# Gate and up products of an adaLN block with retention, block attention and a convolved feed-forward: one 512-column product for high and low tokens, and exits spread over steps

## The chip, the cores and the metric

The kernel runs on one core of one Trainium2 chip, in one launch. The metric is device time in microseconds for one execution, read from the chip, as the median of several runs. All tensors are float32 at the borders. The chip's engines appear under these names: PE (TensorE, products), PEld (its weight loads), DVE (VectorE), ACT (ScalarE), POOL (GpSimd), SP (SyncE, which issues most DMA transfers).

## The reference

One block over 256 tokens of width 1024: a modulation computed from `c`, a token mixer (attention and retention, gated and projected), a layer norm, a feed-forward of width 2816 with a causal filter of three taps over the tokens, and a second layer norm. The change lies in the feed-forward:

```python
def conv_ffn(h, w_ff_gate, w_ff_up, ff_conv_w, ff_conv_b, w_ff_down):
    s = h.shape[1]
    g = h @ w_ff_gate
    u = h @ w_ff_up
    gp = jnp.pad(g, ((0, 0), (CONV_WIDTH - 1, 0), (0, 0)))
    g_conv = sum(gp[:, j:j + s, :] * ff_conv_w[j] for j in range(CONV_WIDTH)) + ff_conv_b
    a = jax.nn.gelu(g_conv, approximate=False) * u
    return a @ w_ff_down

def reference(...):
        ...
        x = layer_norm(DEEPNORM_ALPHA * x + g1 * y, ln1_g[l], ln1_b[l])
        h = x * (1.0 + sc2) + sh2
        y = conv_ffn(h, w_ff_gate[l], w_ff_up[l], ff_conv_w[l], ff_conv_b[l], w_ff_down[l])
        x = layer_norm(DEEPNORM_ALPHA * x + g2 * y, ln2_g[l], ln2_b[l])
```

## The kernel before

**Three products for one.** The products run in a rounded 32-bit type (`float32r`). To keep precision, each operand is split into a high part (rounded) and a low part (what the rounding lost), and `mm3` (L80) sums three products in one PSUM bank: high by high (L81), then the two mixed ones (L82, L83). The product of the two low parts is left out.

**Weights.** A list `main` holds the big weights in units of 128 x 2048 in the order of use. SP loads a unit into one of four `raw` buffers (`load_raw`, L70, issue on L74). Each unit has two halves of 128 x 1024. `prep_halves` splits a half: ACT writes `whi` (L1028), DVE writes `wlo` as raw minus `whi` (L1042); there are eight pairs of these (`HL_BUFS`). Once both halves of a raw buffer are split, the next load into it is issued.

**Steps.** `steps` is a list in which every step uses one half, or a few of them. The main loop at the end (from the line `for s, (need, rel, fn) in enumerate(steps)`) writes out the order of instructions by hand: for each step it advances side work, prepares halves as long as pairs are free (up to eight ahead), and then calls the step's function, which issues the products and, behind them, what takes the result out of the bank. Each engine works through its own queue in this order. In the feed-forward the side work is the scaling of the first norm's output for the second residual (L985), and the products of the last part of the modulation on DVE (`ada`, L154).

**Rounds.** The 2816 features of the feed-forward are 11 rounds of 256. In a round the gate weights and the up weights are stationary: a half has eight blocks of 128 x 128, index k over the 1024 inputs, and the tokens, 256 columns, stream through. `wstat8` (L306) puts the two halves of a unit in the two halves of one of four banks (P0 to P3, taken in turn by `one_bank`). For rounds 0 and 1 the up products run the other way round, with tokens stationary, before the rounds begin. The order of the units is: gate 0, gate 1, then gate r and up r, from round 2 on followed by the down unit of the round before (r = 2: down 0 and down 1) until round 7; rounds 8 to 10 have gate and up alone. The last four down units (rounds 7 to 10) follow as a tail: four steps for the first 128 tokens, one for each round, then three steps for the other 128. The down products have the features stationary and stream 512 columns of weights into banks P4 to P7.

**Exits.** After a gate unit, `gate_done` (L605) lets ACT compute tap 2 and the bias from the bank (L612, once for each half of 128 features), DVE add taps 1 and 0 (L615, four instructions), and ACT take Gelu (L617). After an up unit, `act_in` (L623) multiplies the bank by the gate's result on DVE (L625), and splits the product into `ah` (ACT, L66) and `al` (DVE, L67), the stationary operands of the down unit. All of these are issued at once behind the unit's last product.

**Tokens.** The high and low tokens of the feed-forward lie in four buffers A3a, A3b (high, k 0 to 3 and 4 to 7) and A6a, A6b (low). Earlier stages use the same buffers for other things: input columns, rotated queries and keys, `rv`, the mixer's output; the tail uses A6a and A6b as scratch.

Of the kernel before, what the change touches and what calls it, by code (L numbers as in the profile page):

```python
# [7 lines left out]
F32 = mybir.dt.float32  # L8
F32R = mybir.dt.float32r
AF = mybir.ActivationFunctionType  # L10
OP = mybir.AluOpType
# [17 lines left out]
T0_AT, XN, PRIME = 4, 256, 3  # L29
W0, W1, W2 = (4, 5), (6,), (7,)  # L30
PIECES = dict(ada1=[(0, 512, 1024, 2048)] + [2] * 3 + [1] * 4, winA=[4] * 2 + [2] * 2 + [1] * 4, winX=[1] * 2)
CHUNK = 2
BUSY = 3
SEQ = [(s[0], int(s[1])) for s in
# [17 lines left out]
def _body(nc, a, out, pe, act, dve, sp, cst, wts, big, tmp, ps, dram):  # L52
    f = lambda ap: ap.bitcast(F32)

    def bank(i):
        return ps.tile([128, 512], F32, tag=f"P{i}", name=f"P{i}")

    def slot(n, shape, dt=F32):
        return big.tile(shape, dt, tag=f"A{n}", name=f"A{n}")

    def halves(n):

        return [slot(n + e, [128, 4, 256], F32R) for e in "ab"]
# [16 lines left out]
    def mm3(o, lh, ll, rh, rl, start, stop):  # L80
        pe.matmul(o, lh, rh, start=start, stop=False)  # L81
        pe.matmul(o, lh, rl, start=False, stop=False)  # L82
        pe.matmul(o, ll, rh, start=False, stop=stop)  # L83

    def table(func):

        d_ = tmp.tile([128, 1], F32, name="dummy", bufs=1)
        act.activation(d_, epst, func)
# [7 lines left out]
    consts = {}  # L96
# [5 lines left out]
    bcol = first[:, 136:].rearrange("p (s j) -> p s j", s=6)  # L102
    mod = cst.tile([128, 6, 8], F32, name="mod")

    raws = {}
    loads_A = [(dict(a="ada1", W="winA", X="winX")[n], j) for n, j in SEQ if n in "aWX"]

# [141 lines left out]
    main = []  # L249
# [41 lines left out]
    def one_bank():  # L291
        i = bank_i[0]
        bank_i[0] = (i + 1) % 4
        return bank(i)
# [11 lines left out]
    def wstat8(name, u, xh, xl, done, mid=None):  # L306
        get = lazy(one_bank)

        def mk(half):
            def mm(hi, lo):  # L310
                if half and mid:
                    mid()
                p = get()
                for k in range(8):
                    mm3(p[:, half * 256:half * 256 + 256], hi[:, k * 128:(k + 1) * 128],
                        lo[:, k * 128:(k + 1) * 128], xh(k), xl(k), k == 0, k == 7)
                if half:
                    done(p)
            return mm
        weights(a[name][u], mk(0), mk(1))  # L320

    def wstat4(name, u, xh, xl, done):
# [9 lines left out]
            return mm  # L332
        weights(a[name][u], mk(0), mk(1))

    S = {}
    ghh, ghl = (lambda k: hh[:, k]), (lambda k: hl[:, k])

# [200 lines left out]
        weights4(src, [mk(0, 0), mk(0, 1), mk(1, 0), mk(1, 1)], [range(4)] * 4)  # L538

    def out_start():  # L540
        S["h2h"], S["h2l"] = halves("3"), halves("6")
        GB = S["GB"] = tmp.tile([128, 2, 8], F32, name="GB", bufs=1)
        m = mod[:, 2:4]
        lncol = consts["lncol"]
        dve.tensor_tensor(GB[:, 0], lncol[:, 0], m[:, 0], OP.mult)
        dve.tensor_tensor(GB[:, 1], lncol[:, 1], m[:, 0], OP.mult)
        dve.tensor_tensor(GB[:, 1], GB[:, 1], m[:, 1], OP.add)
        table(AF.Sqrt)
# [56 lines left out]
    def gate_done(r):  # L605
        def fn(p):
            g = slot(("5", "15")[r % 2], [128, 2, 256])
            pv = p.rearrange("p (i t) -> p i t", i=2)
            convw = consts["convw"]
            w = lambda n, i: convw[:, n, 2 * r + i:2 * r + i + 1]  # L610
            for i in range(2):
                act.activation(g[:, i], pv[:, i], AF.Identity, scale=w(2, i), bias=w(3, i))  # L612
# [8 lines left out]
        return fn  # L621

    def act_in(r, u):  # L623
        g = S.pop(("gelu", r)).rearrange("p a b -> p (a b)")
        dve.tensor_tensor(g, u, g, OP.mult)  # L625
        ah = slot(("9a", "9b", "10a", "8a")[r % 4], [128, 2, 256], F32R)
        al = slot(("2a", "2b", "4", 0)[r % 4], [128, 2, 256], F32R)
# [42 lines left out]
    def tok0(i):  # L670
        def fn(ts):
            if i == 0:
                table(AF.Sqrt)
            for hf in range(2):
                down(NR - NG + i, 0, hf, ts[hf], BOTH, False, i == NG - 1 and hf == 1)
            if i == NG - 1:
                n = Norm(S["x1"][:, 0], S["g", 1], S["z2"][0], ("6a", "6b"))
                for c, w in BOTH:
                    n.piece(c, w, S["yf"][c // 512])
                S["rows"] = out_rows(n, 0, BOTH)  # L680
                next(S["rows"])
        return fn

    def tok1(c, w):
# [21 lines left out]
                    pass  # L706
        return fn

    def ffn_gate(r):
        wstat8("wgate", r, gh2, gl2, gate_done(r))  # L710

    def ffn_up(r):
        wstat8("wup", r - 2, gh2, gl2, up_done(r))

    def first():
        bank_i[0] = 0
# [175 lines left out]
    def retention():  # L892
# [50 lines left out]
        for g in range(HR + 1):  # L943
            yield
            if g:
                for t in range(2):
                    act.activation(yr[t][:, c], yr[t][:, c], AF.Copy, scale=sd[:, 2 * g + t - 2:2 * g + t - 1])
            if g < HR:
                c = slice(g * 256, (g + 1) * 256)
                for t in range(2):  # L950
                    dve.scalar_tensor_tensor(yr[t][:, c], yr[t][:, c], mv[:, 2 * g + t, 0:1], srg[t][:, c],
                                             op0=OP.subtract, op1=OP.mult)
            yield
            yield
        yrh, yrl = halves("3"), halves("6")
        S["yrh"], S["yrl"] = yrh, yrl
        for _ in range(3):
# [111 lines left out]
    def run_sides():  # L1069
        for g in list(sides):  # L1070
            if next(g, StopIteration) is StopIteration:
                sides.remove(g)

    for s, (need, rel, fn) in enumerate(steps):
        S["main"] = s
        if s == LN1_AT + 8:
            sides.append(residual())
        run_sides()
        prep_to(max(need) + 1, True)
        late = LN1_AT < s < LN1_AT + 8  # L1080
        if not late:
            prep_to(max(need) + 1 + (LOOKAHEAD if s < LN1_AT - 1 else HL_BUFS))
        run_sides()
        fn([tiles[h] for h in need])
        for h in rel:
            tiles.pop(h)
            live[0] -= 1
        while s % 2 and later and later[0][0] <= s:
            later.pop(0)[1]()
        run_sides()  # L1090
        if late and s >= LN1_AT + PRIME:
            if s == LN1_AT + PRIME:
                next(pg)
            elif s > LN1_AT + 4:
                prep_to(max(need) + 1 + HL_BUFS)
# [90 lines left out]
```

## Time and profile before

| | |
|---|---|
| median of 3 runs | 437.45 us (437.12 to 437.57) |
| the profiled execution's own time | 437.32 us |
| span of the profiled execution, first to last instruction | 435.5 us |
| mean granted TensorE clock | 0.997 |
| DMA | 105.72 MB, mean 243 GB/s |

The span is what the profiler's timeline covers; the profiled execution's own time is 1.8 us longer than its span. In a row of a view that groups instructions stand the line of the kernel, the engine, the operation, output<-inputs with their shapes, the count, the busy time and mean duration of one, and the idle time of the engine just before such instructions with what ended it. In a view of waits stand who waited for whom, the total, how often, and the longest. Products on PE overlap, so the mean duration of one is longer than the distance between two starts.

### The profile page before, as it was taken

To read this page: it belongs to the slowest core of one execution; us is meant where nothing else is said; L and a number is where in the kernel's file an instruction comes from. 1 tells how busy PE (TensorE), PEld (TensorE's weight loads), DVE (VectorE), ACT (ScalarE), POOL (GpSimd) and SP (SyncE) were. 2 spreads that over 40 slices of the span, in tenths; PEclk is the share of its full clock that TensorE was granted. 3 is DMA by queue.
4 is the path that set the end of the run, shared out by engine and by line. 5 is a ranking of instruction groups with operands and counts; after the bars stand their busy time and mean duration, and the time that the engine had idled before them with its cause. 6 is when DMAs were issued, how large, how long until landed. Compare 5 with 4: busy or idle time off the path is not lost.

```text
span 435.5 us, 6921 instructions
## 1 busy us (share of the span) xinstructions
PE 422.5 (97%) x2738; PEld 379.0 (87%) x2738; DVE 346.1 (79%) x550; ACT 241.7 (55%) x369; POOL 6.7 (2%) x16
## 2 busy tenths in 40 slices
PE   5999999999999999999999999999999999999993
PEld 2768888877788999999989899899999999999882
DVE  4979689979997999697779887798886665577476
ACT  4466578579774477543453995655445545355500
POOL 0000000100000000000000010000000000000000
PEclk9999999999999999999999999999999999999998
DMA  8999887787468778779672079577766784550001
GB/s 263 412 423 355 319 322 292 304 339 250 147 275 299 289 288 298 279 286 316 236 267 108 0 255 401 186 267 257 278 238 251 288 274 160 195 193 2 2 24 72
DMA packets 19696, 105.72 MB, mean 243 GB/s; under 512 B 2512, under 2 KB 4560, under 8 KB 8784
## 3 DMA queue, kind: packets, MB, share of 16 engines
q1 hardware_dynamic: 18288, 100.29, 62.1%
q0 software_dynamic: 1376, 4.99, 3.4%
q8 instruction: 21, 0.34, 0.3%
q14 instruction: 11, 0.09, 0.1%
HBM read 104.22 MB, written 1.06 MB: 242 GB/s over the span
## 4 chain that ended last, share of the span: by engine, by line
PE 92%; DMA 4%; DVE 2%; issue 1%; ACT 0%; SPq 0%; DVEq 0%
PE P L81 28%; PE P L82 28%; PE P L83 28%; DMA raw<-in_strm 3%; DMA A3b<-in_strm 1%; PE P L532 1%; PE P L534 1%; PE P L535 1%; PE P L776 1%; PE P L828 1%; PE P L847 1%; PE P L871 1%; DVE junk L154 1%; DVE wlo L67 0%; PE P L917 0%
## 5 line engine op out<-in xcount | busy, mean ns | idle before, releaser
L1042 DVE TENSOR_TENSOR wlo<-raw,whi 128x1024 fp32r<-128x1024 f32 x118 | 140.4, 1219 | 24.7 <-ACT whi L1028 24.7
L1028 ACT ACTIVATE whi<-raw 128x1024 fp32r<-128x1024 f32 x118 | 120.2, 1051 | 41.3 <-PE P L83 12.4
L83 PE MATMUL P<-whi,A 128*128 128x512 f32 (+1 forms) x212 | 80.3, 379 | 0.0
L81 PE MATMUL P<-whi,A 128*128 128x512 f32 (+1 forms) x168 | 65.4, 389 | 0.1
L82 PE MATMUL P<-wlo,A 128*128 128x512 f32 (+1 forms) x168 | 64.0, 381 | 0.5 <-DVE wlo L67 0.5
L154 DVE CUSTOM_DVE_ANT_0 junk<-raw,srow 128x1024 bf16<-128x1024 f32 (+1 forms) x49 | 58.7, 1197 | 3.5 <-ACT srow L141 1.8
L81 PE MATMUL P<-A3a,whi 128*128 128x256 f32 x192 | 54.4, 283 | 0.0
L81 PE MATMUL P<-A3b,whi 128*128 128x256 f32 x192 | 54.3, 283 | 0.0
L82 PE MATMUL P<-A6b,whi 128*128 128x256 f32 x192 | 54.3, 283 | 0.0
L83 PE MATMUL P<-A3b,wlo 128*128 128x256 f32 x192 | 54.3, 283 | 0.0
L83 PE MATMUL P<-A3a,wlo 128*128 128x256 f32 x192 | 54.3, 283 | 0.0
L82 PE MATMUL P<-A6a,whi 128*128 128x256 f32 x192 | 54.3, 283 | 0.0
L83 PEld LDWEIGHTS P<-whi,A 128*128 128x128 f32 x212 | 39.9, 188 | 7.9
L81 PE MATMUL P<-A,whi 128*128 128x256 f32 x160 | 45.9, 287 | 0.0
L83 PE MATMUL P<-A,wlo 128*128 128x256 f32 x160 | 45.2, 283 | 0.0
L82 PE MATMUL P<-A,whi 128*128 128x256 f32 x160 | 45.2, 283 | 0.0
L81 PEld LDWEIGHTS P<-whi,A 128*128 128x128 f32 x168 | 31.6, 188 | 7.1 <-issue 1.3
L82 PEld LDWEIGHTS P<-wlo,A 128*128 128x128 f32 x168 | 31.7, 188 | 6.7 <-DVE wlo L67 1.2
L82 PEld LDWEIGHTS P<-A6a,whi 128*128 128x128 f32 x192 | 36.8, 192 | 0.3
L81 PEld LDWEIGHTS P<-A3a,whi 128*128 128x128 f32 x192 | 36.8, 192 | 0.3
L81 PEld LDWEIGHTS P<-A3b,whi 128*128 128x128 f32 x192 | 36.9, 192 | 0.0
L82 PEld LDWEIGHTS P<-A6b,whi 128*128 128x128 f32 x192 | 36.9, 192 | 0.0
(235 smaller groups left out, 734.0 us busy)
## 6 DMA issues: line engine op xcount, KB each, us to landing
raw<-in_ada SPq DMA_DIRECT2D x16, 1024.0 KB, 5.2
raw<-in_wup SPq DMA_DIRECT2D x11, 1024.0 KB, 4.8
raw<-in_wgate SPq DMA_DIRECT2D x11, 1024.0 KB, 5.1
raw<-in_wdown SPq DMA_DIRECT2D x11, 1024.0 KB, 4.9
raw<-in_winB SPq DMA_DIRECT2D x10, 1024.0 KB, 5.8
raw<-in_strm SPq DMA_DIRECT2D x8, 1024.0 KB, 6.6
raw<-in_strm SPq DMA_DIRECT2D x11, 512.0 KB, 7.2
raw<-in_winGr SPq DMA_DIRECT2D x4, 1024.0 KB, 6.0
```

Source lines behind the costliest of these rows:

```text
L81: pe.matmul(o, lh, rh, start=start, stop=False)
L82: pe.matmul(o, lh, rl, start=False, stop=False)
L83: pe.matmul(o, ll, rh, start=False, stop=stop)
L154: dve.tensor_tensor_reduce(out=junk[:, rows], in0=raw[:, rows], in1=srow[:, rows], scale=1.0, scalar=0.0, op0=OP.mult, op1=OP.add, accum_o ...
L532: pe.matmul(p, xl(k)[:, tk], hi[:, c], start=False, stop=k == 7)
L534: pe.matmul(p, xh(k)[:, tk], hi[:, c], start=k == 0, stop=False)
L535: pe.matmul(p, xh(k)[:, tk], lo[:, c], start=False, stop=False)
L776: pe.transpose(p[:, i * 128:(i + 1) * 128], roped[:, which * 512 + i * 128:which * 512 + (i + 1) * 128], ident)
L828: pe.matmul(ps2[e][:, c], qkT[0][s, h // 2, qb * 128:(qb + 1) * 128], qkT[1][s, h // 2, :128 + 128 * qb], start=True, stop=True)
L847: pe.matmul(p[64 * e:64 * e + 64, o], v[:, kb, 64 * (h + e):64 * (h + e) + 64], pT[e][:, c], start=kb == 0, stop=kb == 1)
L1028: act.activation(hi, src, AF.Copy)
L1042: dve.tensor_tensor(lo, src, f(hi), OP.subtract)
```

## The change

In rounds 3 to 10 the gate and up products of a half are issued by `wstat8m` and `mm2` in place of `wstat8` and `mm3`. For this the high and low tokens of a k must be reachable by one access pattern: the four buffers A3a, A3b, A6a, A6b become two, Ya (A3a and A6a) and Yb (A3b and A6b), of 128 x 2 x 1024, and earlier uses take a half of them. `mm2` sends the high weights of k once against 512 columns (256 high tokens, 256 low tokens), and the low weights against the 256 high tokens, added to the first 256 columns of the bank. So a half fills a whole bank, and its result is the sum of the bank's two halves.

The exit of a half: ACT copies the second half of the bank to the buffer at once; at the next step DVE adds the first half. For the gate, DVE then computes all three taps from the buffer (tap 2 with the bias as a new instruction on DVE), and Gelu follows on ACT one step later. For up, DVE multiplies after the second half's addition, ACT writes `ah` one step later and DVE `al` two steps later. Deferred parts are put into a list (`put_off`) and issued in the main loop behind that step's split of weights and ahead of its products. The gate's buffer A5 or A15 now also holds the copied results and has four blocks of 256 for two. Rounds 0 to 2 keep their code.

```diff
+MERGED = 3
...
+    place = {"3a": ("Ya", 0), "6a": ("Ya", 1), "3b": ("Yb", 0), "6b": ("Yb", 1)}
+    pairs = {}
+
+    def reopen(dt, *names):
+        for n in names:
+            pairs[n] = big.tile([128, 2, 1024], dt, tag=f"A{n}", name=f"A{n}")
...
     def slot(n, shape, dt=F32):
-        return big.tile(shape, dt, tag=f"A{n}", name=f"A{n}")
+        if n not in place:
+            return big.tile(shape, dt, tag=f"A{n}", name=f"A{n}")
+        pair, e = place[n]
+        assert pairs[pair].dtype == dt
+        v = pairs[pair][:, e, :math.prod(shape[1:])]
+        return v.rearrange("p (a b) -> p a b", a=shape[1]) if len(shape) == 3 else v
...
+    def mm2(o, wh, wl, x2, start, stop):
+        if start:
+            pe.matmul(o, wh, x2, start=True, stop=False)
+        pe.matmul(o[:, :256], wl, x2[:, 0], start=False, stop=False)
+        if not start:
+            pe.matmul(o, wh, x2, start=False, stop=stop)
...
+    def wstat8m(name, u, x2, copy, done):
+        def mk(half):
+            def mm(hi, lo):
+                p = one_bank()
+                for k in range(8):
+                    mm2(p, hi[:, k * 128:(k + 1) * 128], lo[:, k * 128:(k + 1) * 128], x2(k), k == 0, k == 7)
+                t = copy(half)
+                act.activation(t, p[:, 256:], AF.Copy)
+
+                def rest():
+                    dve.tensor_tensor(t, p[:, :256], t, OP.add)
+                    done(half)
+                put_off(1, rest)
+            return mm
+        weights(a[name][u], mk(0), mk(1))
+
+    waiting = []
+
+    def put_off(n, fn):
+        waiting.append((S["main"] + n, fn))
...
     def out_start():
-        S["h2h"], S["h2l"] = halves("3"), halves("6")
+        S["h2"] = [slot("Y" + e, [128, 2, 4, 256], F32R) for e in "ab"]
+        S["h2h"], S["h2l"] = [[t[:, i] for t in S["h2"]] for i in range(2)]
...
+    def gu(r):
+        if ("gu", r) not in S:
+            S["gu", r] = slot(("5", "15")[r % 2], [128, 4, 256])
+        return S["gu", r]
+
+    def gate_done_m(r):
+        def fn(half):
+            g, x = gu(r)[:, half], gu(r)[:, 2 + half]
+            convw = consts["convw"]
+            w = lambda n: convw[:, n, 2 * r + half:2 * r + half + 1]
+            dve.tensor_scalar(g, x, w(2), w(3), op0=OP.mult, op1=OP.add)
+            for n in (1, 0):
+                dve.scalar_tensor_tensor(g[:, 2 - n:], x[:, :254 + n], w(n), g[:, 2 - n:],
+                                         op0=OP.mult, op1=OP.add)
+            if half:
+                put_off(1, lambda: act.activation(gu(r)[:, :2], gu(r)[:, :2], AF.Gelu))
+        return fn
+
+    def up_done_m(r):
+        def fn(half):
+            if half:
+                g = gu(r)[:, :2]
+                dve.tensor_tensor(g, gu(r)[:, 2:], g, OP.mult)
+                ah, al = S["a", r] = a_slots(r)
+                put_off(1, lambda: act.activation(ah, g, AF.Copy))
+                put_off(2, lambda: dve.tensor_tensor(al, g, f(ah), OP.subtract))
+        return fn
...
+    h2 = lambda k: S["h2"][k // 4][:, :, k % 4]
+
     def ffn_gate(r):
-        wstat8("wgate", r, gh2, gl2, gate_done(r))
+        if r < MERGED:
+            wstat8("wgate", r, gh2, gl2, gate_done(r))
+        else:
+            wstat8m("wgate", r, h2, lambda half: gu(r)[:, 2 + half], gate_done_m(r))
 
     def ffn_up(r):
-        wstat8("wup", r - 2, gh2, gl2, up_done(r))
+        if r < MERGED:
+            wstat8("wup", r - 2, gh2, gl2, up_done(r))
+        else:
+            wstat8m("wup", r - 2, h2, lambda half: gu(r)[:, 2 + half], up_done_m(r))
...
         run_sides()
+        for e in waiting:
+            if e[0] <= s:
+                e[1]()
+        waiting[:] = [e for e in waiting if e[0] > s]
         fn([tiles[h] for h in need])
```

The diff also moves the choice of the `ah` and `al` buffers into a function `a_slots`, and calls `reopen` at three places: at the start (`F32`), before the mixer's output is transposed (`F32R`), and at the head of the tail's norm (`F32`), which together give the paired buffers their type.

More of the change, by code (lines that the diff above doesn't have):

```diff
@@ L103, in _body @@
     mod = cst.tile([128, 6, 8], F32, name="mod")
+    reopen(F32, "Ya", "Yb")
     raws = {}
@@ L621, in gate_done, with a_slots @@
         return fn
+    def gu(r):
[23 more added lines that the diff above has]
+        return fn
+    def a_slots(r):
+        return (slot(("9a", "9b", "10a", "8a")[r % 4], [128, 2, 256], F32R),
+                slot(("2a", "2b", "4", 0)[r % 4], [128, 2, 256], F32R))
     def act_in(r, u):
@@ L625, in act_in @@
         dve.tensor_tensor(g, u, g, OP.mult)
-        ah = slot(("9a", "9b", "10a", "8a")[r % 4], [128, 2, 256], F32R)
-        al = slot(("2a", "2b", "4", 0)[r % 4], [128, 2, 256], F32R)
+        ah, al = a_slots(r)
         split(ah.rearrange("p a b -> p (a b)"), al.rearrange("p a b -> p (a b)"), g)
@@ L676, in fn @@
             if i == NG - 1:
+                reopen(F32, "Ya", "Yb")
                 n = Norm(S["x1"][:, 0], S["g", 1], S["z2"][0], ("6a", "6b"))
@@ L954, in retention @@
             yield
+        reopen(F32R, "Ya", "Yb")
         yrh, yrl = halves("3"), halves("6")
```

## The prediction

> **What bounds the kernel now.** I read the page first, then who waited for whom on TensorE, then the start times of single products in the changed rounds, then the busy time of each engine round by round. On the page, the span, TensorE's busy row and the chain that ended last by engine:
>
> ```profile
> span 435.5 us, 6921 instructions
> PE 422.5 (97%) x2738; PEld 379.0 (87%) x2738; DVE 346.1 (79%) x550; ACT 241.7 (55%) x369; POOL 6.7 (2%) x16
> ...
> PE 92%; DMA 4%; DVE 2%; issue 1%; ACT 0%; SPq 0%; DVEq 0%
> ```
>
> Nearly the whole chain is TensorE. The view of its waits has four rows for the entire kernel:
>
> ```profile
> PE P L139 <- DVE sc L132: 3.2, 1, 3.2
> PE P L204 <- DVE A L189: 1.1, 1, 1.1
> PE P L82 <- DVE wlo L67: 0.5, 2, 0.3
> PE P L204 <- ACT A L176: 0.5, 1, 0.5
> ```
>
> All four name lines of the opening stage (L132, L189, L67 on `wlo`, L176); no row names a line of the feed-forward rounds. There TensorE waits for nobody, so time is bought there only by giving it less to do, and is lost only if a new wait appears.
>
> How much less is read from start to start, not from the duration of one product, since neighbours overlap. In the timeline of TensorE, the columns are start, duration, engine, line; rows around the down step of round 3 (24 products of 512 columns between gate and up products of 256), then two rows of rounds 8 to 10, which are 256-column products without a break:
>
> ```profile
> 314.74 0.40 PE L81 MATMUL P<-whi,A8a 128*128 128x512 f32 x1
> 314.98 0.40 PE L82 MATMUL P<-wlo,A8a 128*128 128x512 f32 x1
> 315.21 0.39 PE L83 MATMUL P<-whi,A 128*128 128x512 f32 x1
> ...
> 315.90 0.39 PE L83 MATMUL P<-whi,A 128*128 128x512 f32 x1
> ...
> 320.21 0.28 PE L81 MATMUL P<-A3a,whi 128*128 128x256 f32 x1
> 320.32 0.28 PE L82 MATMUL P<-A6a,whi 128*128 128x256 f32 x1
> 320.44 0.28 PE L83 MATMUL P<-A3a,wlo 128*128 128x256 f32 x1
> ...
> 371.38 0.28 PE L83 MATMUL P<-A3a,wlo 128*128 128x256 f32 x1
> ...
> 405.70 0.40 PE L81 MATMUL P<-whi,A8a 128*128 128x512 f32 x1
> ```
>
> Narrow (256 columns): from 371.38 to 405.70 lie 286 products, 34.32 / 286 = 0.120 us each. Wide (512): from 315.90 to 320.21 lie 19, 4.31 / 19 = 0.227 us each. Twice the columns cost 0.107 more, so about 0.013 us of each product does not depend on its width. The rows also show the two changes of width: the first two wide products after a narrow run take (315.21 - 314.74) / 2 = 0.235, and the first narrow one after a wide run takes 0.11 (320.21 to 320.32), the next 0.12.
>
> **The change part by part.** *The products.* A half (128 output features, eight indices k) is 24 narrow products now: per k, 3 x 0.120 = 0.360 us. Afterwards k takes one wide product (high weights by high and low tokens) and one narrow one (low weights by high tokens). Rounds 3 to 10 hold 8 rounds x 2 matrices x 2 halves x 8 = 256 such k, so 256 products go, and in the built instruction order exactly these. At the steady rates k costs 0.227 + 0.120 = 0.347, a saving of 0.013 x 256 = 3.3 us.
>
> Nowhere in this trace do wide and narrow alternate, so the price has bounds from the rows at the changes of width. If every narrow one takes what the first after a wide one takes (0.11; I take 0.113, between it and the 0.115 mean of two), k costs 0.340 and 256 x 0.020 = 5.1 us go. If every wide one takes the 0.235 of the first ones and the narrow ones keep 0.120, k costs 0.355 and 1.3 us go. With first wide and first narrow together it is 0.235 + 0.113 = 0.348, again the middle. I take 0.347 and keep 5.1 and 1.3 as ends.
>
> The Trainium skill speaks against so much: "TensorE: Matmul & The Clock Gate", Back-to-back issue gap, puts a warm product at its columns over 2.4 GHz plus 2.5 ns, by which joining two saves 2.5 ns, an estimate of 0.6 us over 256. The rows above say 13 ns (2 x 120 - 227), so I sum by the rows.
>
> The moving operand of a wide product is now two pieces of 256 that lie 1,024 elements apart; every wide product in this trace reads one piece. The nearest row is still the wide one. The lower end is zero saving, the two pieces costing two narrow products, 0.240.
>
> *The exits.* Per half ScalarE copies the low-token half out of the bank and, a step later, VectorE adds the other half. The gate's first filter step moves from ScalarE (two per round) to VectorE; the later filter steps, Gelu, product, and the split into `ah` and `al` stay, later in the queues. The nearest groups (last columns: busy us, mean ns, idle before):
>
> ```profile
> L612 ACT ACTIVATE A<-P,convw 128x256 f32<-128x256 f32 x22 | 11.2, 559 | 14.5 <-PE P L83 14.5
> L921 ACT ACTIVATE A8a<-P 128x256 f32<-128x256 f32 x4 | 1.5, 379 | 4.9 <-PE P L919 4.9
> L67 DVE TENSOR_TENSOR A<-P,A 128x256 fp32r<-128x256 f32 x4 | 1.7, 417 | 0.8 <-ACT A L66 0.8
> L468 DVE TENSOR_SCALAR A<-A,mv,sd 128x768 f32<-128x768 f32 x2 | 1.3, 671 | 0.0
> L625 DVE TENSOR_TENSOR A<-P,A 128x512 f32<-128x512 f32 x9 | 6.2, 683 | 0.0
> ```
>
> ScalarE, per round: four copies at 0.38 less two filter steps at 0.56, +0.4 us. VectorE: four adds at 0.42, and two filter steps that no row shows at this size, below the 0.67 of 768 columns; I take 0.42. That is +2.5 us (at most 4 x 0.68 + 2 x 0.67 = 4.1). All of it lies beside TensorE as long as VectorE keeps up. Its busy time in five rounds of 17.0 us, and in one of the last three rounds, which have no down step:
>
> ```profile
> core 0: us, PE busy (x) PEld busy (x) DVE busy (x) ACT busy (x) POOL busy (x), PEclk, DMA share, GB/s
> 288.00:305.00 17.00, 17.00 (x122) 16.04 (x121) 15.13 (x21) 8.20 (x10) 0.00 (x0) 1.00 0.74 270
> 305.00:322.00 17.00, 17.00 (x122) 16.04 (x121) 14.17 (x22) 8.20 (x10) 0.00 (x0) 1.00 0.71 253
> 322.00:339.00 17.00, 17.00 (x123) 16.04 (x122) 13.11 (x20) 8.21 (x10) 0.00 (x0) 1.00 0.69 255
> 339.00:356.00 17.00, 17.00 (x123) 16.04 (x122) 11.62 (x16) 8.20 (x10) 1.08 (x2) 1.00 0.78 281
> 356.00:373.00 17.00, 17.00 (x123) 16.04 (x122) 10.14 (x13) 8.20 (x10) 0.00 (x0) 1.00 0.54 185
> ...
> 384.50:396.00 11.50, 11.50 (x99) 11.50 (x98) 7.67 (x10) 6.08 (x8) 0.00 (x0) 1.00 0.45 176
> ```
>
> A half will take 8 x 0.347 = 2.78 us, a round with its down step 4 x 2.78 + 24 x 0.227 = 16.6, one without it 11.1. VectorE then needs 15.13 + 2.5 = 17.6 in round 3 (1.0 late), 16.7 in round 4 (0.1 more), 15.6 and less afterwards, 10.2 of 11.1 at the end. At the upper price of 4.1 it is 2.6, 1.7 and 0.6 late in rounds 3 to 5, together 4.9.
>
> Who would feel it? *Weights:* the eight `whi`/`wlo` pairs are refilled as soon as a half has let go of its pair, seven halves, 19 us, ahead of use. *Banks:* a half now owns one of the four banks alone, and gives it back only after VectorE's add; TensorE asks for it again four merged halves later. In rounds 8 to 10 three halves lie between, 8.3 us; with a down step between it is five. *The new waits on TensorE* (29 in the built order, one for VectorE at nearly every merged half) stand ahead of all later products, and are met with those 8.3 us in hand. *Loads:* the order on the DMA queues is unchanged and no deferred exit issues a transfer; a late split delays a reload, but four raw buffers lie ahead of the eight pairs.
>
> *The end of round 10* has the least cover. The last exit must deliver `ah` and `al` before the fourth down group of the tail, after 3 x 12 x 0.227 = 8.2 us. A table load and the old last links, in the timeline:
>
> ```profile
> 408.28 0.69 DVE L67 TENSOR_TENSOR A<-A,A10a 128x512 fp32r<-128x512 f32 x1 [0.76 <-ACT A10a L66]
> ...
> 409.21 1.28 ACT L88 ACT_TABLE_LOAD   x1
> ```
>
> Afterwards the chain is copy 0.38, add 0.42, product 0.68, then on ScalarE a weight split (some 1.0) and this table load 1.28 ahead of `ah` 0.63, then `al` 0.69: about 4.5 us with hand-overs. It fits, with some 3.7 to spare.
>
> *The rest* costs nothing: the paired buffers for tokens are reopened at the same points and the order up to round 3 is the same on every engine.
>
> **The sum.** The profiled execution took 437.32 us (435.5 span and 1.8 around it), 0.13 under the median of 437.45. 437.32 - 3.3 = 434.0 us.
>
> **The rivals.** *A, narrow products recover:* with a wide neighbour on each side, each narrow product keeps the first one's 0.113. 437.3 - 5.1 = 432.2. For it: the 0.11 above. Against: the wide ones after a narrow run pay more than their steady rate.
>
> *B, each change of width is paid:* 0.235 for wide and 0.120 for narrow, 437.3 - 1.3 = 436.0. For it: the slow first wide products. Against: that slowness has gone by 315.90, five products on.
>
> *C, the joining saves nothing:* the change does not do what it says, because a two-piece operand costs two narrow products. 437.3. No row tests it. The fixed cost that the Trainium skill's page gives would land close by, at an estimated 436.7; the trace so far bears its 2.5 ns out nowhere in these rounds.
>
> *D, VectorE becomes the bound (slower):* at the banks of rounds 8 to 10, if it keeps the idle time it has now on top of its 2.5 us. All of it kept, it falls 17.0 + 2.5 - 16.6 = 2.9 behind in each of five rounds and 11.5 + 2.5 - 11.1 = 2.9 in three, 23 us; beyond 8.3 of cover TensorE waits. Two thirds of this (15.5) cost 7.2 us: 441.2. It is slower than before once the lag passes 8.3 + 3.3 = 11.6. For it: one queue in strict order with four more waits on TensorE's halves per round. Against it, the waits of these rounds:
>
> ```profile
> DVE wlo L1042 <- ACT whi L1028: 22.8, 23, 1.7
> ACT whi L1028 <- PE P L82: 8.5, 5, 1.7
> ACT whi L1028 <- PE P L83: 6.4, 6, 1.2
> ```
>
> VectorE idles because it is early: it waits for ScalarE, which waits for TensorE to let go of a pair. A late engine does not wait there.
>
> **How the numbers follow.** Forecast 0.57, A 0.17, B 0.12, C 0.06, D 0.08. The likeliest gives 434.0. 432.0 to 436.2 takes in the forecast, A and B, and leaves 0.14 out for C and D. What a measurement here can tell from no change is 0.2%, 0.9 us: faster is below 436.6, which forecast, A and B reach, but B only just, so 0.84; C and a piece of B are the same, 0.08; slower is D, 0.08.
>
> **What would show it.** Right: 256 products fewer on TensorE, a start-to-start of 0.347 us per pair in rounds 3 to 10, a half of 2.78 instead of 2.88 us, no new row in TensorE's waits, VectorE at most a few microseconds later, and the last product some 3.3 us earlier than now. A pair of 0.340 is A, 0.355 is B, 0.360 is C. Wrong in kind: a row that lets TensorE wait for VectorE's add, for `ah` or `al` of round 10, or for `wlo` in rounds 3 to 10; then D holds, and the stall is as long as VectorE's lag beyond its cover.

## The result, and the profile after

| | before | after |
|---|---|---|
| median of 6 runs each | 437.42 us (436.94 to 438.02) | 434.26 us (433.82 to 434.82) |
| ratio after to before, 95% interval | | 0.9931 (0.9919 to 0.9943) |
| the profiled execution's own time | 437.32 us | 434.37 us |
| span of the profiled execution | 435.5 us | 432.6 us |
| TensorE, from the last transposition ahead of the rounds to the start of the last product | 172.60 us | 169.81 us |
| mean of the 32 halves of rounds 3 to 10, first product to the next product behind the half | 2.879 us | 2.796 us |

The kernel became 0.7% faster; 434.0 was forecast. The stretch in the table's fifth row is the part of the kernel that the change touches. It came out as 169.813 us in four of the profiled executions shown here, while the opening before it varied by about 1.1 us from run to run. So single times scatter by half a microsecond or more, and small differences below are read from this stretch.

On the page of after: the span, the engines' busy row and the chain that ended last by engine.

```profile
span 432.6 us, 6504 instructions
PE 420.6 (97%) x2482; PEld 365.0 (84%) x2482; DVE 365.5 (84%) x598; ACT 244.0 (56%) x385; POOL 6.7 (2%) x16
...
PE 92%; DVE 3%; DMA 3%; issue 1%; ACT 0%; SPq 0%; DVEq 0%
```

TensorE has 256 products fewer (2738 to 2482) and is still nearly the whole chain. VectorE has 48 instructions and 19 us more. Who waited for whom on TensorE, for the entire kernel:

```profile
PE P L164 <- DVE sc L157: 3.1, 1, 3.1
PE P L97 <- DVE wlo L82: 0.5, 2, 0.3
PE P L229 <- DVE A L214: 0.4, 1, 0.4
PE P L229 <- ACT A L201: 0.2, 1, 0.2
```

These are the four rows that stood there before, under new line numbers (L164 was L139, L97 was L82, L229 was L204). None names L104, L105 or L107, the lines of `mm2`: no new wait arose. The timeline of TensorE shows two halves of round 3 and the first product of the down step behind them (start, duration, engine, line):

```profile
291.71 0.39 PE L104 MATMUL P<-AYa,whi 128*128 128x512 f32 x1
291.94 0.40 PE L105 MATMUL P<-AYa,wlo 128*128 128x256 f32 x2
292.18 0.40 PE L107 MATMUL P<-AYa,whi 128*128 128x512 f32 x1
...
294.30 0.40 PE L107 MATMUL P<-AYb,whi 128*128 128x512 f32 x1
294.53 0.40 PE L104 MATMUL P<-AYa,whi 128*128 128x512 f32 x1
...
294.99 0.40 PE L107 MATMUL P<-AYa,whi 128*128 128x512 f32 x1
...
297.07 0.40 PE L107 MATMUL P<-AYb,whi 128*128 128x512 f32 x1
297.31 0.39 PE L96 MATMUL P<-whi,A10a 128*128 128x512 f32 x1
```

The first half takes 294.53 - 291.71 = 2.82 us, the second 297.31 - 294.53 = 2.78. Inside, six pairs of a wide and a narrow product take (294.30 - 292.18) / 6 = 0.353 in the first and (297.07 - 294.99) / 6 = 0.347 in the second. All rounds show these two beats: 2.815 on average for the first half of a unit, 2.777 for the second. The forecast was 0.347 and 2.78 for both.

Busy time of each engine, round by round, as before (now 16.6 us with a down step, 11.1 without):

```profile
288.00:304.60 16.60, 16.60 (x90) 14.23 (x89) 16.35 (x26) 8.28 (x12) 0.00 (x0) 1.00 0.77 287
304.60:321.20 16.60, 16.60 (x90) 14.22 (x89) 16.35 (x26) 8.44 (x13) 0.00 (x0) 1.00 0.70 255
321.20:337.80 16.60, 16.60 (x90) 14.22 (x89) 15.90 (x26) 8.67 (x13) 0.00 (x0) 1.00 0.70 274
337.80:354.40 16.60, 16.60 (x90) 14.22 (x89) 14.13 (x23) 8.52 (x12) 1.08 (x2) 1.00 0.78 298
354.40:371.00 16.60, 16.60 (x89) 14.23 (x88) 12.54 (x19) 8.62 (x12) 0.00 (x0) 1.00 0.51 194
...
382.10:393.20 11.10, 11.10 (x66) 9.66 (x65) 10.02 (x16) 6.20 (x10) 0.00 (x0) 1.00 0.27 97
```

TensorE is busy throughout at the full clock. VectorE (the third busy time, behind those of PE and PEld) is nearly full in the first two rounds, 16.35 of 16.60. Its new instructions and ScalarE's copy, as groups of rounds 3 to 10 (last columns: busy us, mean ns of one, idle before):

```profile
L372 DVE TENSOR_TENSOR A<-P,A 128x256 f32<-128x256 f32 x31 | 13.0, 418 | 0.0
L684 DVE TENSOR_SCALAR A<-A,convw 128x256 f32<-128x256 f32 x16 | 6.6, 413 | 0.6
L369 ACT ACTIVATE A<-P 128x256 f32<-128x256 f32 x32 | 12.2, 382 | 36.3 <-PE P L107 30.2 <-DVE A L686 6.1
```

They cost what the prediction took for them: 0.42, 0.42 and 0.38.

### The profile page after: what moved, and what is told of

It reads as the page before. It is cut to its first block, busy times and chain, and to the rows that moved or that the text cites. A ratio compares the mean times of both kernels' runs of the same rounds, so it can differ in the third digit from the quotient of the medians.

```text
span 432.6 us, 6504 instructions
## 1 busy us (share of the span) xinstructions
PE 420.6 (97%) x2482; PEld 365.0 (84%) x2482; DVE 365.5 (84%) x598; ACT 244.0 (56%) x385; POOL 6.7 (2%) x16
## 4 chain that ended last, share of the span: by engine, by line
PE 92%; DVE 3%; DMA 3%; issue 1%; ACT 0%; SPq 0%; DVEq 0%
PE P L96 21%; PE P L97 21%; PE P L98 21%; PE P L107 12%; PE P L105 7%; DMA raw<-in_strm 3%; PE P L104 2%; DVE junk L179 1%; DVE wlo L82 1%; PE P L581 1%; PE P L583 1%; PE P L584 1%; PE P L867 1%; PE P L919 1%; PE P L938 1%
## 5 line engine op out<-in xcount | busy, mean ns | idle before, releaser
L1120 ACT ACTIVATE whi<-raw 128x1024 fp32r<-128x1024 f32 x118 | 121.6, 1053 | 28.7 <-PE P L98 8.8
L96 PE MATMUL P<-whi,A 128*128 128x512 f32 (+1 forms) x168 | 65.3, 389 | 0.1
L97 PE MATMUL P<-wlo,A 128*128 128x512 f32 (+1 forms) x168 | 64.0, 381 | 0.5 <-DVE wlo L82 0.5
L107 PE MATMUL P<-AYb,whi 128*128 128x512 f32 x128 | 46.2, 396 | 0.0
L96 PE MATMUL P<-A,whi 128*128 128x256 f32 x160 | 45.9, 287 | 0.0
L97 PE MATMUL P<-A,whi 128*128 128x256 f32 x160 | 45.2, 283 | 0.0
L96 PEld LDWEIGHTS P<-whi,A 128*128 128x128 f32 x168 | 31.6, 188 | 7.2 <-issue 1.3
L97 PEld LDWEIGHTS P<-wlo,A 128*128 128x128 f32 x168 | 31.7, 188 | 6.7 <-DVE wlo L82 1.3
L105 PE MATMUL P<-AYb,wlo 128*128 128x256 f32 x128 | 35.6, 278 | 0.0
L107 PE MATMUL P<-AYa,whi 128*128 128x512 f32 x96 | 35.2, 396 | 0.0
L369 ACT ACTIVATE A<-P 128x256 f32<-128x256 f32 x32 | 12.2, 382 | 36.3 <-PE P L107 30.2
L82 DVE TENSOR_TENSOR wlo<-raw,whi 128x1024 fp32r<-128x1024 f32 (+1 forms) x24 | 24.5, 1044 | 8.6 <-ACT whi L81 8.1
L96 PEld LDWEIGHTS P<-A,whi 128*128 128x128 f32 x160 | 30.6, 192 | 0.5 <-issue 0.4
L97 PEld LDWEIGHTS P<-A,whi 128*128 128x128 f32 x160 | 30.7, 192 | 0.0
L98 PEld LDWEIGHTS P<-A,wlo 128*128 128x128 f32 x160 | 30.7, 192 | 0.0
L105 PE MATMUL P<-AYa,wlo 128*128 128x256 f32 x128 | 30.5, 279 | 0.0
L107 PEld LDWEIGHTS P<-AYb,whi 128*128 128x128 f32 x128 | 24.0, 188 | 5.8
```

Of the source, the lines that this page charges most:

```text
L82: dve.tensor_tensor(lo, src, f(hi), OP.subtract)
L105: pe.matmul(o[:, :256], wl, x2[:, 0], start=False, stop=False)
L107: pe.matmul(o, wh, x2, start=False, stop=stop)
L369: act.activation(t, p[:, 256:], AF.Copy)
L1120: act.activation(hi, src, AF.Copy)
```

## The experiments

Twelve kernels ran, each a small edit of the changed one. The stretch is the fifth row of the table above, taken from the one profiled execution of each, which in e2 took 0.7 us more than the median and in e7 1.5 us less; ratios are to the kernel before, with their 95% intervals.

| run | median us | ratio | stretch us |
|---|---|---|---|
| the change | 434.26 | 0.9931 (0.9919 to 0.9943) | 169.813 |
| e1_three_narrow | 436.75 | 0.9990 (0.9982 to 0.9999) | 172.380 |
| e3_one_piece | 434.41 | 0.9935 (0.9923 to 0.9948) | 169.813 |
| e4_grouped | 434.06 | 0.9930 (0.9917 to 0.9942) | 169.707 |
| e5_strict_turns, one run | 435.58 | | 171.006 |
| e6_other_bank, one run | 434.16 | | 169.813 |
| e2_exits_at_once | 439.38 | 1.0048 (1.0034 to 1.0061) | 175.587 |
| e11_gelu_at_once | 436.80 | 0.9998 (0.9988 to 1.0008) | 172.413 |
| e10_only_gelu_later | 434.55 | 0.9943 (0.9931 to 0.9955) | 169.813 |
| e7_one_more_add | 439.29 | 1.0053 (1.0039 to 1.0068) | 173.740 |
| e8_two_more_adds | 455.07 | 1.0411 (1.0398 to 1.0425) | 189.979 |
| e12_all_rounds | 435.27 | 0.9948 (0.9933 to 0.9963) | 170.243 |
| e13_grouped_and_round2 | 434.37 | 0.9929 (0.9913 to 0.9944) | 169.360 |

### Does the joining itself bring the time?

**e1_three_narrow** takes the wide product apart again, for every k but the first, and leaves banks, exits and their places as in the change.

```diff
-            pe.matmul(o, wh, x2, start=False, stop=stop)
+            pe.matmul(o[:, :256], wh, x2[:, 0], start=False, stop=False)
+            pe.matmul(o[:, 256:], wh, x2[:, 1], start=False, stop=stop)
```

> The new exits stay as the change made them, but from the second index on each wide product is taken apart again into two narrow ones (23 products a half for 16). Theory (the gain is the price of the products alone, the exits are hidden): a half costs 0.347 + 7 x 0.360 = 2.87 us, 32 halves save 0.4 against before, so 437.0 us. Rival (the gain came from the exits being spread over steps): near the changed kernel, 434.3 to 434.8 us.

A half took 2.871 us and the kernel 436.75: the gain is gone, but for the first k, which stays joined ((2.879 - 2.871) x 32 = 0.3 us). So the products bring it and the exits bring nothing. It also shows that the exits as the change places them cost nothing, as no wait stands on TensorE in these rounds.

**e3_one_piece** lays the tokens out so that the 512 columns of a k lie side by side.

```diff
-        S["h2"] = [slot("Y" + e, [128, 2, 4, 256], F32R) for e in "ab"]
+        S["h2"] = [slot("Y" + e, [128, 4, 2, 256], F32R) for e in "ab"]
...
-    h2 = lambda k: S["h2"][k // 4][:, :, k % 4]
+    h2 = lambda k: S["h2"][k // 4][:, k % 4]
```

> High and low tokens of an index lie side by side, so that a wide product reads one piece of 512 columns instead of two of 256. Theory (the price of a pair, 0.350 us in the trace of the changed kernel, comes from the change of width): 434.3 us, halves of 2.78 to 2.82 us as before. Rival (the two pieces cost the 6 to 14 ns that a wide product takes beyond 0.227): a half falls to 8 x (0.227 + 0.115) = 2.74 us and 32 x 0.06 = 1.9 us go, 432.4 us.

Nothing changed: the stretch is the same to the nanosecond, and so, to a nanosecond, are the two beats (2.815 and 2.777). Two pieces of 256 stream at the rate of one of 512. Rival C had rested on the opposite, and falls by both runs.

### What does a change of width cost?

**e4_grouped** issues the eight wide products of a half first, then the eight narrow ones: two changes of width per half where the change has fourteen.

```diff
+                ks = [slice(k * 128, (k + 1) * 128) for k in range(8)]
                 for k in range(8):
-                    mm2(p, hi[:, k * 128:(k + 1) * 128], lo[:, k * 128:(k + 1) * 128], x2(k), k == 0, k == 7)
+                    pe.matmul(p, hi[:, ks[k]], x2(k), start=k == 0, stop=False)
+                for k in range(8):
+                    pe.matmul(p[:, :256], lo[:, ks[k]], x2(k)[:, 0], start=False, stop=k == 7)
```

> Within a half all eight wide products come first, then all eight narrow ones. If every change of width has a price of its own, two changes a half cost little and the half comes to 8 x 0.227 + 8 x 0.120 = 2.776 us, 32 x 0.02 = 0.6 us less than the changed kernel: 433.6 us. If a wide product is slow for about five products after a narrow run, as at the down steps of the kernel before (26 ns in all, against 8 ns that the first narrow ones gain), the half comes to 2.79 us and the time stays at 434.2 us. If a narrow product is cheaper only beside a wide one, the half is dearer than 2.80.

Half by half it is 2.793 or 2.794, with 2.766 for a half behind a down step; the mean is 2.788, against 2.796. The timeline of TensorE in round 4 (each row stands for several products, the last column):

```profile
308.09 1.09 PE L368 MATMUL P<-AYa,whi 128*128 128x512 f32 x4
309.02 1.07 PE L368 MATMUL P<-AYb,whi 128*128 128x512 f32 x4
309.94 0.64 PE L370 MATMUL P<-AYa,wlo 128*128 128x256 f32 x4
310.41 0.64 PE L370 MATMUL P<-AYb,wlo 128*128 128x256 f32 x4
310.89 1.09 PE L368 MATMUL P<-AYa,whi 128*128 128x512 f32 x4
```

The wide ones take 0.93 / 4 = 0.233 and 0.92 / 4 = 0.230 each, slower than the 0.227 of a long run; the narrow ones 0.47 / 4 = 0.118 and then 0.120. A half at the steady rates would take 8 x 0.227 + 8 x 0.120 = 2.776. A half behind a down step follows other wide products and lacks the entry into them: so the entry into narrow ones gives 2.776 - 2.766 = 0.010 back, and the entry into wide ones costs 2.794 - 2.766 = 0.028. Two changes cost 0.018 a half. Yet fourteen of them cost only 0.020 on average in the change, so the price does not add up change by change.

**e5_strict_turns** drops the swap that `mm2` makes from the second k on: wide, narrow, wide, narrow throughout, also across halves.

```diff
-        if start:
-            pe.matmul(o, wh, x2, start=True, stop=False)
-        pe.matmul(o[:, :256], wl, x2[:, 0], start=False, stop=False)
-        if not start:
-            pe.matmul(o, wh, x2, start=False, stop=stop)
+        pe.matmul(o, wh, x2, start=start, stop=False)
+        pe.matmul(o[:, :256], wl, x2[:, 0], start=False, stop=stop)
```

> Within a half wide and narrow products strictly take turns, wide first for every index, so that no two of a kind are neighbours. If the 2.815 and 2.777 us of odd and even halves come from the doubled narrow product at the start of each half, all halves take the same; if they do not, the two lengths stay. 434.0 to 434.6 us either way.

A half takes 2.82 on average (2.810 to 2.831), a pair 0.353, and the stretch is 1.2 us longer than the change's. This is a single execution, but the stretch elsewhere repeats to the nanosecond. The two beats are gone: within a round the halves behind the first take 2.83, 2.83 and 2.82, and from pair to pair the starts lie 0.350, 0.361 and 0.349 apart, over and over.

**e6_other_bank** skips one bank ahead of round 3, so that the first half of a unit lands in another bank than before.

```diff
+                if not S.get("skipped"):
+                    S["skipped"] = one_bank
+                    one_bank()
                 p = one_bank()
```

> One bank is skipped ahead of round 3, so that first halves get the banks which second halves had. If the bank makes the difference between 2.815 and 2.777 us, the long halves are now the second ones; if not, they stay the first ones. 434.3 us either way.

The long half stays the first of a unit (2.815, then 2.777). The two beats come neither from the bank nor, by e3, from the layout of the tokens. They hang on the order of the products, since neither e4 nor e5 shows them; how is open.

### Is VectorE the next bound, and how far off?

**e7_one_more_add** and **e8_two_more_adds** put one, and two, more VectorE products of 256 columns ahead of each addition. What they write is used by nothing.

```diff
+                    junk = tmp.tile([128, 1024], mybir.dt.bfloat16, name="junk", bufs=1)
+                    for _ in range(1):
+                        dve.tensor_tensor(junk[:, :256], t, t, OP.mult)
                     dve.tensor_tensor(t, p[:, :256], t, OP.add)
```

(In e8 the loop runs over `range(2)`.)

> One idle VectorE product of 256 columns (some 0.45 us) is added in each of the 32 exits; its result is used by nothing. VectorE then needs 19.4, 18.5, 17.4, 15.9 and 14.4 us in rounds 3 to 7 of 16.6, and 12.0 of 11.1 after them. Theory (lag costs nothing until it passes the cover of the banks, 8.3 us in rounds 8 to 10 and 13.8 before): the lag grows from 5 to some 10 and comes to the cover at the end only: 434.3 to 436.5 us, and any wait of TensorE lies in rounds 8 to 10. Rival (the change already stands at the edge, each microsecond more on VectorE shows in the time): 32 x 0.45 = 14 us more, 448 us.

> Two such idle products in each exit, 3.6 us a round. VectorE then needs 21.2, 20.3, 19.2, 17.7, 16.2 of 16.6 and 13.8 of 11.1 three times. Theory (as before): the lag passes the cover, and what is beyond shows: about 16 us, 450 us, with TensorE waiting for VectorE's addition. Rival (waiting queues feed on each other and it costs more than the sum): above 455; or the cover is larger than worked out: below 442.

One more already costs 5.0 us (439.29 against 434.26), beyond what was expected; the trace, of an execution of 437.77, shows only part of the loss. TensorE's waits there from round 3 on:

```profile
PE P L96 <- ACT A10a L701: 1.6, 1, 1.6
PE P L104 <- DVE A L375: 0.7, 2, 0.5
PE P L104 <- ACT A L369: 0.4, 1, 0.4
```

With two more, the three largest rows of TensorE's waits in the rounds and the tail are these:

```profile
PE P L104 <- DVE A L375: 6.4, 4, 3.1
PE P L96 <- ACT A10a L701: 3.9, 1, 3.9
PE P L98 <- DVE A2a L702: 2.2, 1, 2.2
```

The first two are rows that the prediction named for rival D: L104 starts a half and waits for the addition (L375) that frees its bank, L96 in the tail waits for `ah` of round 10. The third, `al` of round 4 late for its down step, it had not named. Together they hold 12.5 us of the 20.2 by which the stretch grew. Much of the rest is the clock, since TensorE's rate falls after each of the three longest stalls (granted clock 0.71, 0.75 and 0.66 in the windows of five microseconds behind them). Windows of e8 around the first of these (PEclk is the third number from the end):

```profile
330.00:335.00 5.00, 2.79 (x12) 2.00 (x11) 4.97 (x8) 1.54 (x3) 0.00 (x0) 0.94 0.48 156
335.00:340.00 5.00, 5.00 (x17) 3.95 (x16) 4.61 (x10) 1.33 (x2) 0.00 (x0) 0.71 0.74 280
```

TensorE stands for 2.2 of the first five microseconds, and in the next five, though busy throughout, it starts only 17 products, at a granted clock of 0.71. So D's mechanism is real, and the banks of the last rounds are among its places. In the change itself the addition ends 3.1 to 4.1 us after its half in rounds 7 to 10, and the bank is free 4.3 to 5.3 us before TensorE wants it in rounds 8 to 10; of 8.3 us of cover, about half is left. One product of 0.4 us more per half uses it up, because VectorE's lag adds up: in e7 the addition ends 5.4 us after the first half of round 3, up to 11.6 after a half of round 6, and still 8 to 9 in rounds 9 and 10.

### What is the later issue worth?

The prediction costed the exits' places at nothing. **e2_exits_at_once** issues all of an exit directly behind its half.

```diff
-        waiting.append((S["main"] + n, fn))
+        fn()
```

> The wide products stay, but every deferred part of an exit is issued at once, behind the last product of its half. Theory (the exits are off the path as long as VectorE's lag stays below the cover of the banks, 8.3 us at the least): 434.3 us, no new row in TensorE's waits. Rival (the deferral is what keeps VectorE and ScalarE from blocking behind TensorE): TensorE waits for weights or banks in rounds 3 to 10, above 436 us.

It took 439.38, slower than before. TensorE's waits in the rounds and the tail:

```profile
PE P L96 <- ACT A10a L698: 1.8, 1, 1.8
PE P L104 <- DVE A L372: 1.4, 1, 1.4
```

The cause is on ScalarE. Its timeline in e2, in round 9 (the number in brackets is the idle time before the instruction, and what ended it):

```profile
395.46 0.63 ACT L689 ACTIVATE A<-A 128x512 f32<-128x512 f32 x1 [4.58 <-DVE A L686]
396.00 1.04 ACT L1120 ACTIVATE whi<-raw 128x1024 fp32r<-128x1024 f32 x1
396.95 0.36 ACT L369 ACTIVATE A<-P 128x256 f32<-128x256 f32 x1
```

and VectorE's there:

```profile
394.42 1.00 DVE L686 SCALAR_TENSOR_TENSOR A<-A,convw 128x255 f32<-128x255 f32 x2
397.07 1.23 DVE L1134 TENSOR_TENSOR wlo<-raw,whi 128x1024 fp32r<-128x1024 f32 x1 [1.65 <-ACT whi L1120]
```

Gelu (L689) stands at the head of ScalarE's queue and waits 4.58 us for VectorE's filter steps (L686). Behind it stand the weight split `whi` (L1120) and the next copy (L369). VectorE finishes the filter and then waits 1.65 us for that same `whi`. So each engine waits for the other in turn, and the lag grows until the bank is late. The same row of waits in after, then in e2:

```profile
ACT A L689 <- DVE A L686: 10.2, 8, 2.2
```

```profile
ACT A L689 <- DVE A L686: 46.1, 8, 8.1
```

Two runs place the blame on Gelu alone. **e11_gelu_at_once** is the change with Gelu issued directly behind the filter steps, one step earlier:

```diff
-                put_off(1, lambda: act.activation(gu(r)[:, :2], gu(r)[:, :2], AF.Gelu))
+                act.activation(gu(r)[:, :2], gu(r)[:, :2], AF.Gelu)
```

> As the changed kernel, but Gelu is issued directly behind the filter steps of its gate, one step earlier than in the change; all else is deferred as there. Theory (ScalarE blocked behind Gelu by VectorE's lag of some 5 us is what costs): ScalarE waits for VectorE's filter steps clearly longer than the 10.2 us of the changed kernel, and the time is 436 to 439 us. Rival (one step of deferral of the rest is enough): 434.3 us.

**e10_only_gelu_later** issues everything at once, as e2, but Gelu two steps later, where the change has it:

```diff
-        waiting.append((S["main"] + n, fn))
+        fn()
+
+    def later_on(n, fn):
+        waiting.append((S["main"] + n, fn))
...
-                put_off(1, lambda: act.activation(gu(r)[:, :2], gu(r)[:, :2], AF.Gelu))
+                later_on(2, lambda: act.activation(gu(r)[:, :2], gu(r)[:, :2], AF.Gelu))
```

> As the run with all exits at once, but Gelu alone keeps the place that the change gives it, two steps behind its half. In that run ScalarE stood 46 us in front of Gelu waiting for VectorE's filter steps. Theory (it is this one place in ScalarE's queue that makes the stall): 434.3 to 435.3 us, no wait of TensorE for a bank. Rival (the additions and splits at once block as much): 437 us or more.

e11 lost the whole gain (436.80, its row of waits for Gelu 48.1 us), e10 kept it (434.55, the stretch identical to the change's). The other deferred parts are worth nothing measurable; Gelu's place is worth 2.5 us (e11 against the change) when the rest is deferred, 4.8 us (e2 against e10) when it is not.

### Can more rounds be merged?

**e12_all_rounds** merges gates 0 and 1 and round 2 as well. The parts of its diff that are not shown let `wstat8m` carry the transpositions in the middle of gate 0, and issue the exits of rounds 0 and 1 behind their Gelu.

```diff
-MERGED = 3
+MERGED = 0
...
-    wstat8("wgate", 0, gh2, gl2, gate_done(0), first)
+    wstat8m("wgate", 0, h2, lambda half: gu(0)[:, 2 + half], gate_done_m(0), first)
```

> The gates of rounds 0 and 1 and gate and up of round 2 are merged as well: eight halves more. Theory (each saves 2.88 - 2.796 = 0.084 us): 0.7 us less than the changed kernel, 433.6 us. Rival (VectorE, which splits a row of nine halves of weights at the start of these rounds, is late there and TensorE waits): 434.3 us or more, with a row of TensorE's waits.

435.27 by the median, and the stretch is 0.43 longer than the change's though 64 more products are gone. VectorE's timeline at the start of the rounds:

```profile
255.79 5.77 DVE L1142 TENSOR_TENSOR wlo<-raw,whi 128x1024 fp32r<-128x1024 f32 x5 [1.53 <-ACT whi L1128]
261.47 0.42 DVE L374 TENSOR_TENSOR A<-P,A 128x256 f32<-128x256 f32 x1
```

It splits weights ahead for the rounds, five without a break (four more lie just before), and the first addition (L374) stands behind them. TensorE waits for the bank:

```profile
PE P L104 <- DVE A L374: 0.7, 1, 0.7
```

Seven of the eight further halves lie in the stretch, and at 0.083 each they save 0.6. So the stall costs some 0.6 + 0.4 = 1.0 (an estimate), more than its wait of 0.7.

**e13_grouped_and_round2** takes the products of e4 and merges round 2 alone (`MERGED = 2`).

> Grouped order (eight wide, then eight narrow products a half), and gate and up of round 2 merged as well, but the gates of rounds 0 and 1 as before. Theory: 36 halves at 2.79 us for 32 at 2.796 and 4 at 2.88, 0.19 + 0.36 = 0.5 us less than the changed kernel, 433.7 us, no new row in TensorE's waits. Rival (VectorE comes into round 3 with more lag and reaches the cover of the banks): 434.3 us or more and a wait for VectorE's addition.

The stretch is 0.45 us shorter than the change's, as was worked out, with no new wait, but the median of 434.37 cannot be told from the change's 434.26. By the medians, no version that ran is measurably faster than the change.

## Why the prediction was right, point by point

**The sum.** 437.32 - 3.3 = 434.0 was forecast; the profiled execution took 434.37. The mis-sized term is the one for the products, 0.013 x 256 = 3.3: the trace gives (2.879 - 2.796) x 32 = 2.6 for the halves. The stretch adds 0.14 that the prediction left out: the six groups of down products that stand behind gate or up products now follow a wide product and start at the steady rate (24 of them take 5.444 us where they took 5.468). Together that is the 2.8 of the stretch; the medians differ by 3.2, and what lies beyond 2.8 is within the scatter of single times. Per k it is 0.3495 where 0.347 was forecast, so a removed product saves 0.083 / 8 = 0.0103 us.

**Between A and B.** The step that failed is the reading that the wide product's slowness "has gone by 315.90, five products on" and so does not count. Over all halves a wide product is followed by the next after 0.234 and a narrow one after 0.116. So wide ones are dearer, as B said, and narrow ones cheaper, as A said, at the same time. The alternative that the prediction had itself noted, "first wide and first narrow together", 0.235 + 0.113 = 0.348, was the right way to read the rows and misses by 0.002. That the steady rates came so close is in part luck: 7 ns more on the wide product and 4 ns less on the narrow one nearly cancel.

**The rule of the Trainium skill.** The Trainium skill, "TensorE: Matmul & The Clock Gate", Back-to-back issue gap, would have had 2.5 ns saved per removed product, an estimate of 0.6 us in all; that section gives the 2.5 ns for a product taken by itself and says that in a stream the weight loads set the spacing too. The 10.3 ns of the halves decide against the 2.5 for these products, each of which brings its own weights.

**C** is refuted by e1 and e3. **The exits** cost what the nearest rows said (the three groups above). VectorE's work in the five long rounds grew from 64.2 to 75.3 us (sums of the windows' rows), 2.2 per round where 2.5 was forecast. ScalarE's copies came to 12.2 us.

**Banks and D.** "8.3 us in hand" is right, and e8 shows that this is what decides. But the prediction set only VectorE's lateness of about a microsecond against it. The addition also lies behind the next step's weight split by the change's own order, and uses 3.1 to 4.1 us of the cover in the last rounds (up to 5.8 in rounds 3 and 4, where five halves lie between). D did not come, but was nearer than the text made it look: one product of 0.4 us per half, or one step in Gelu's place, brings it about.

**Order within the queues.** "Stay, later in the queues" was costed at nothing, and that holds for the kernel as changed. What was not asked is what the later place buys: without it the same arithmetic is 0.5% slower than before (e2). The prediction saw the queue whose order mattered, and that VectorE and ScalarE wait for each other, but sought the danger in VectorE's four new waits for TensorE a round, not in an activation that waits at the head of ScalarE's queue.

**The end of round 10.** The chain takes 5.5 us instead of 4.5, and runs over another engine than foretold. VectorE's and then ScalarE's timeline there; the last half ends at 402.81:

```profile
404.60 1.23 DVE L1134 TENSOR_TENSOR wlo<-raw,whi 128x1024 fp32r<-128x1024 f32 x1 [0.45 <-ACT whi L1120]
405.74 0.42 DVE L372 TENSOR_TENSOR A<-P,A 128x256 f32<-128x256 f32 x1
...
407.59 0.69 DVE L699 TENSOR_TENSOR A<-A,A10a 128x512 fp32r<-128x512 f32 x1 [0.70 <-ACT A10a L698]
```

```profile
404.59 1.28 ACT L112 ACT_TABLE_LOAD   x1
...
406.92 0.63 ACT L698 ACTIVATE A10a<-A 128x512 fp32r<-128x512 f32 x1 [0.84 <-DVE A L696]
```

The table load, which the prediction put on the path, is over at 405.87, while VectorE is still at work: it waits for a weight split and does its own half of it ahead of the last addition. `al` is ready at 408.28. The fourth down group starts at 410.98, so 2.7 us are to spare instead of 3.7.

## What to carry to other kernels

Joining two products that share their weights saves the fixed part of one product, here 10 ns of 120, and only if the exits that it makes heavier stay inside the time that their bank is lent; work that time out with everything that stands ahead of the exit in its engine's queue. An instruction that waits for a slower engine should be issued when its input is ready, not when it is logically next: one early Gelu held up weight splits and copies behind it, and cost nearly as much as the joining brought. Where widths alternate, read the price from the first products after each change, both kinds together, not from the steady rate of either.

## What the runs showed of the hardware that was not expected

**Half clock after a short stall.** The timeline of TensorE in e2, at the wait for `ah` of round 10:

```profile
414.60 0.50 PE L96 MATMUL P<-whi,A10a 128*128 128x512 f32 x1 [1.76 <-ACT A10a L698]
...
416.21 0.63 PE L98 MATMUL P<-whi,A 128*128 128x512 f32 x1
416.63 0.63 PE L96 MATMUL P<-whi,A10a 128*128 128x512 f32 x1
417.06 0.63 PE L97 MATMUL P<-wlo,A10a 128*128 128x512 f32 x1
```

and its window:

```profile
415.00:420.00 5.00, 5.00 (x15) 3.61 (x14) 3.28 (x5) 1.99 (x3) 0.00 (x0) 0.66 0.00 0
```

After 1.76 us of idling, wide products start 0.42 to 0.43 apart instead of 0.227, from 1.6 us behind the stall, and the granted clock of that window is 0.66. Waits of up to 1.6 us in e11, e2, e7 and e8 were not followed by it, those of 2.2 us and more in e8 were. The longest that was not, 1.65 us in e7, lies near 1.76, and each stands in a single execution, so these runs give no exact limit. The Trainium skill, "TensorE: Matmul & The Clock Gate", Part 1 on the clock gate, names an idle window of about 3.4 us for the fall to half rate; here half of that was enough. The fall makes a stall dearer than its length: the stretch of e2 is 5.8 us longer than the change's, while its two waits come to 3.2. Not all of that is the clock. From the first down product behind round 10 to the last product it takes 21.96 us in the change, 24.17 in e7 with the wait of 1.65 us, and 26.05 in e2 with that of 1.76. So a stall at full clock already costs 0.6 more than its wait, and the fallen clock some 1.8 on top.

**The price of mixed widths does not add up.** Two changes of width in a half cost 18 ns (e4), fourteen cost 20 on average (the change), and sixteen, in strict turns, 48 (e5). So it is not the number of changes alone that counts. Why the first half of each unit takes 2.815 and the second 2.777 was not found, beyond that it needs the change's order of products.
